# Seven-product blocks in a second FFN of a two-layer diffusion trunk, and the modulation stream over three FFNs

## The chip, the cores and the metric

The kernel runs on one core of one Trainium2 chip. The metric is device time in microseconds (us) of one execution. The kernel before has a median of 1832.51 us over 3 runs (1830.86 to 1833.24).

## The reference

There are two layers. Each has 256 latent tokens and 256 context tokens of width 1024, all in f32, and does the following with shared weights:

```
mod = silu(c) @ ada_w[layer] + ada_b[layer]            # 9 rows of 1024, one set per stream
x   = x + 0.5 * mod[2] * swiglu(ada_rms(x, mod[0], mod[1]))      # FFN 0, width 2816
hx  = ada_rms(x, mod[3], mod[4])
x   = x + mod[5] * mixer(hx, hc)     # neighbourhood attention, gMLP gate, retention
x   = x + 0.5 * mod[8] * swiglu(ada_rms(x, mod[6], mod[7]))      # FFN 1
swiglu(h) = (silu(h @ w1[:, :2816]) * (h @ w1[:, 2816:])) @ w2
```

The context stream goes through the same steps, with its own modulation, up to the mixer of the second layer; only the latent stream is returned. So the second layer needs modulation rows 0 to 4 for both streams, and rows 5 to 8 for one.

## The kernel before

All weights are f32 in memory. A matmul in f32r is made exact enough by splitting each operand into a high and a low part: a weight chunk of 128 x 1024 is loaded into `wr` by SP, copied to `wh` by ScalarE (line 87), and `wl = wr - wh` is made by VectorE (line 98). Each product is then three matmuls: high by high, high by low, low by high (lines 204 to 206). `Stream` (`ws`) keeps three `wr`, four `wh` and four `wl`, and `take` writes the casts and subtractions of two to three chunks ahead of the matmuls that use them.

Names for the stages: FFN (l, f) is FFN f of layer l. Each runs in two halves of eleven blocks. A half has an up stage (eleven blocks j, each one gate and one up column block, 128 columns by 1024 deep, for 512 tokens) and a down stage (eight output tiles m, each of two chunks of 768 and 640 columns). After each m, `residual` (line 429) adds the PSUM result to `xT` on VectorE for the two streams; in the second half `Norm.add` squares the new rows for the next norm (lines 325, 329). In the last half the last two m are split by stream, latent first, and the norm of the latent rows starts (`stats`, line 338, matmuls on PE) while the context half is still running.

The engines' orders are those of the code as it is written (`manual_schedule`). Work that isn't tied to a matmul stands in the list `bg`; `pump` is called after each product and takes `pace[0]` steps from it per 512 columns. `drain_bg` empties it.

FFN (1, 0) computes 18 of its 22 up blocks with `Seven`: the block is a 2 x 2 product (gate and up weights by the two halves of the depth, latent and context tokens), and is made of seven products of half the depth and 256 tokens in place of eight. Its combined weights are made by DMA with accumulation (`add`, on the POOL queue, into `cb`), by POOL (`second`, line 546) and VectorE (`fourth`, line 551), and split as other weights are (lines 531, 540). The four blocks in front (`DIRECT`) are plain, and cover the sums of the activations (`sums`).

The modulation is a stream of matrix-vector products on VectorE: `ada_steps` loads a tile `aw` of 128 x 1024 (512 KB) for each row r and block b, and `step` multiplies and sums it with `cb` (silu of the conditions), once per stream (line 278). A "step" below is one such instruction. Rows 2 to 8 of layer 0 (112 steps) run in FFN (0, 0), all 112 steps of layer 1 in FFN (0, 1). Five `aw` buffers (`ADA_BUFS`) let the load of tile i + 4 be written ahead of step i. The mixer's tables `tab` are loaded once, at the start.

Of the kernel before, what the change touches and what calls it, by code (L numbers as in the profile page):

```python
# [9 lines left out]
F32 = mybir.dt.float32  # L10
# [28 lines left out]
DIRECT = 4  # L39
# [15 lines left out]
APACE = (0.28, 0.26)  # L55
# [77 lines left out]
def tile_hybrid_dit(ctx: ExitStack, tc: tile.TileContext, t_x, t_c, t_cb, t_ada0, t_ada, t_adab, t_nw, t_w1, t_w2,  # L133
# [22 lines left out]
    for l in range(L):  # L156
        for f in range(2):
            if f == 1:
                chunks += [t_wi[l, i] for i in WI[l]] + [t_wo[l, m] for m in range(KT)]
            for half in range(2):  # L160
                for j in range(JH) if (l, f) != (1, 0) else range(DIRECT * (1 - half)):
# [55 lines left out]
    with tc.manual_schedule():  # L217
# [16 lines left out]
        tab = const.tile([128, t_tab.shape[1]], F32, name="tab")  # L234
# [22 lines left out]
        adap = [None]  # L257
        cb = const.tile([128, 2, D], F32, name="cb")

        def ada_steps(l, rounds):  # L260

            todo = [(r, b) for r in rounds for b in range(KT)]
# [10 lines left out]
            def step(i, s, n):  # L273
                loads(i + ADA_BUFS)
                r, b = todo[i]
                t = tiles[r, b]
                junk = adap[0].tile([128, CHUNK], F32, tag="junk", name="junk") if s < n - 1 else t
# [15 lines left out]
            out = [lambda: loads(ADA_BUFS)]  # L293
            for a, r in enumerate(rounds):

                n = 1 if l == L - 1 and r > 4 else 2
                out += [lambda i=a * KT + b, s=s, n=n: step(i, s, n) for b in range(KT) for s in range(n)]
                out.append(lambda r=r, n=n: fin(r, n))
# [149 lines left out]
        class Seven:  # L448
# [8 lines left out]
            def __init__(self, pool, l, f):  # L457
                self.pool, self.l, self.f = pool, l, f
# [4 lines left out]
            def sums(self, q):  # L463
# [3 lines left out]
                def work():  # L467
                    for tag in ("a", "cu", "ur"):
                        x.append(self.pool.tile([128, NT], F32, tag=tag, name="sum", bufs=1).rearrange(
                            "p (k t) -> p k t", k=2))  # L470
# [29 lines left out]
            def load(self, j):  # L500
# [5 lines left out]
                q = cb[:, j % 2]  # L506
# [46 lines left out]
            def prepare(self, j):  # L553
# [4 lines left out]
                        lambda: self.low("r", j)]  # L558
# [15 lines left out]
            def go(self, j, done, nxt):  # L574

                a = self.pool.tile([128, NT], F32, tag="a", name="a", bufs=1)[:, 0:T]
                y = self.pool.tile([128, NT], F32, tag="sg", name="sg", bufs=1)
                w = self.pool.tile([128, NT], F32, tag="cu", name="cu", bufs=1)
# [35 lines left out]
        def ffn(l, f, lead, norms, steps=None, tail=None):  # L614
# [7 lines left out]
            with tc.tile_pool(name="ffn", bufs=1) as fp:  # L622
                adap[0] = fp
                seven = Seven(fp, l, f) if (l, f) == (1, 0) else None
                if seven:
                    caps = [ws.n_take + 2 * DIRECT, ws.n_take + 2 * DIRECT + 2 * KT, len(ws.chunks)]
                    ws.cap = caps[0]
                for half in range(2):
# [34 lines left out]
                    if half == 0 and not one:  # L663
# [10 lines left out]
                        if seven:  # L674
                            bg.extend([s for q in range(2) for s in seven.sums(q)])
                            bg.append(lambda: seven.load_u(DIRECT))
# [8 lines left out]
                    j1 = DIRECT * (1 - half) if seven else JH  # L685
                    if seven and half == 0:
                        seven.load(j1)
                        seven.load(j1 + 1)
                        bg.extend([lambda: seven.add(j1), lambda: seven.add(j1 + 1)])
                        first_j = seven.prepare(j1)  # L690
                    for j in range(j0, j1):
                        if seven and j == j1 - 1:
                            bg.extend(first_j)
# [9 lines left out]
                    if seven:  # L703
                        drain_bg()
                    for j in range(j1, JH if seven else j1):
                        n = half * JH + j

                        def nxt(slot):
                            last_j = j == JH - 1
                            if slot == 1:  # L710
                                seven.high("u", n)
                            if slot == 2:
# [1087 lines left out]
```

## Time and profile before

| | us |
|---|---|
| median of 3 runs | 1832.51 |
| profiled execution, own time | 1833.68 |
| span from its first to last instruction | 1831.9 |
| PE busy in the span | 1802.7 (98%) |
| VectorE busy | 1225.2 (67%) |
| ScalarE busy | 690.0 (38%) |
| POOL busy | 188.0 (10%) |

PE is TensorE's matmuls, DVE is VectorE, ACT is ScalarE. A span is cut into stretches by the stage that runs in it; the busy time of each engine in a stretch tells how much of it is left.

### The profile page before, as it was taken

How to read it: one execution, taken by the hardware profiler on the slowest of the kernel's cores; microseconds unless marked ns; L12 is line 12 of the kernel's file. 1: busy time of each engine (PE TensorE's matmuls, PEld its weight loads, DVE VectorE, ACT ScalarE, POOL GpSimd, SP SyncE). 2: the span in 40 equal slices, each digit the busy share in tenths (PEclk: the TensorE clock that was granted, in tenths of full speed). 3: DMA queues.
4: the chain of work that ended last, by engine and by line, in shares of the span. 5: the costliest groups of instructions: out<-in, count | busy, mean ns of one | idle time of the engine just before them, and what ended most of it. 6: DMA issues, size and time to landing. Idle time of an engine off the chain costs nothing. (4 is left out here: it accounts for less than half of the span.)

```text
span 1831.9 us, 27737 instructions
## 1 busy us (share of the span) xinstructions
PE 1802.7 (98%) x10944; PEld 1534.8 (84%) x10944; DVE 1225.2 (67%) x2064; ACT 690.0 (38%) x1131; POOL 188.0 (10%) x207
## 2 busy tenths in 40 slices
PE   7999999999999999999999999999999999999999
PEld 5788888887668989888888898989998867889999
DVE  5787877756455667877777667846884644566665
ACT  3332222235543234322222234433543555454443
POOL 0000000002024300000000002302320104310000
PEclk9999999999999999999999999999999999999999
DMA  7755655333211124555567425636653432345655
GB/s 287 267 190 185 208 185 198 124 100 115 78 56 58 47 75 153 193 185 182 201 219 266 151 88 150 160 110 175 167 147 96 129 104 77 92 127 182 188 177 156
DMA packets 94242, 277.00 MB, mean 151 GB/s; under 512 B 11040, under 2 KB 17824, under 8 KB 93984
## 3 DMA queue, kind: packets, MB, share of 16 engines
q1 hardware_dynamic: 88928, 265.79, 44.3%
q0 software_dynamic: 5184, 9.44, 3.2%
q8 instruction: 86, 1.41, 0.3%
q14 instruction: 44, 0.36, 0.1%
HBM read 274.14 MB, written 1.05 MB: 150 GB/s over the span
## 5 line engine op out<-in xcount | busy, mean ns | idle before, releaser
L98 DVE TENSOR_TENSOR wl<-wr,wh 128x1024 fp32r<-128x1024 f32 (+1 forms) x340 | 364.5, 1100 | 110.6 <-ACT wh L87 109.1
L87 ACT CAST wh<-wr 128x1024 fp32r<-128x1024 f32 (+1 forms) x340 | 311.8, 945 | 189.2 <-PE d L205 127.6
L204 PE MATMUL d<-aTh,wh 128*128 128x512 f32 (+1 forms) x770 | 268.9, 349 | 0.0
L205 PE MATMUL d<-aTl,wh 128*128 128x512 f32 (+1 forms) x770 | 268.4, 349 | 0.0
L206 PE MATMUL d<-aTh,wl 128*128 128x512 f32 (+1 forms) x770 | 268.4, 349 | 0.0
L204 PE MATMUL g<-hTh,wh 128*128 128x512 f32 (+2 forms) x592 | 208.7, 353 | 2.4 <-ACT wh L87 1.4
L205 PE MATMUL g<-hTl,wh 128*128 128x512 f32 (+2 forms) x592 | 208.4, 352 | 1.3 <-DVE hTl L354 1.1
L206 PE MATMUL g<-hTh,wl 128*128 128x512 f32 (+2 forms) x592 | 207.6, 351 | 1.1 <-DVE wl L98 1.1
L206 PE MATMUL u<-hTh,wl 128*128 128x512 f32 (+2 forms) x592 | 207.4, 350 | 0.4 <-DVE wl L98 0.4
L204 PE MATMUL u<-hTh,wh 128*128 128x512 f32 (+2 forms) x592 | 207.0, 350 | 0.0
L205 PE MATMUL u<-hTl,wh 128*128 128x512 f32 (+2 forms) x592 | 206.9, 349 | 0.0
L205 PEld LDWEIGHTS d<-aTl,wh 128*128 128x128 f32 x770 | 144.5, 188 | 21.3
L204 PEld LDWEIGHTS d<-aTh,wh 128*128 128x128 f32 x770 | 144.5, 188 | 21.2
L206 PEld LDWEIGHTS d<-aTh,wl 128*128 128x128 f32 x770 | 144.5, 188 | 21.2
L278 DVE CUSTOM_DVE_ANT_0 aw<-aw,cb 128x1024 f32<-128x1024 f32 x128 | 155.1, 1223 | 2.4
L652 ACT CAST aTh<-sg 128x512 fp32r<-128x512 f32 x66 | 40.9, 620 | 255.4 <-DVE sg L648 241.7
L212 PE MATMUL nat<-wh,hTh 128*128 128x512 f32 (+2 forms) x384 | 137.1, 357 | 0.0
L429 DVE SCALAR_TENSOR_TENSOR xT<-d,mod,xT 128x256 f32<-128x256 f32 x112 | 50.3, 480 | 122.7 <-PE d L206 122.6
L204 PEld LDWEIGHTS g<-hTh,wh 128*128 128x128 f32 x592 | 111.6, 189 | 20.1 <-ACT wh L87 2.3
L214 PE MATMUL nat<-wh,hTl 128*128 128x512 f32 (+2 forms) x384 | 127.8, 333 | 0.4 <-DVE hTl L354 0.4
L213 PE MATMUL nat<-wl,hTh 128*128 128x512 f32 (+2 forms) x384 | 127.6, 332 | 0.0
L205 PEld LDWEIGHTS g<-hTl,wh 128*128 128x128 f32 x592 | 111.9, 189 | 18.1 <-DVE hTl L354 2.6
(261 smaller groups left out, 3440.4 us busy)
## 6 DMA issues: line engine op xcount, KB each, us to landing
wr<-in_w_dram SPq DMA_DIRECT2D x158, 512.0 KB, 4.3
aw<-in_ada_dram SPq DMA_DIRECT2D x144, 512.0 KB, 5.2
wr<-in_wi_dram SPq DMA_DIRECT2D x56, 512.0 KB, 3.7
wr<-in_w_dram SPq DMA_DIRECT2D x64, 384.0 KB, 3.5
wr<-in_w_dram SPq DMA_DIRECT2D x64, 320.0 KB, 2.9
cb<-in_w_dram SPq DMA_DIRECT2D x36, 256.0 KB, 6.2
cb<-in_w_dram POOLq DMA_DIRECT2D x36, 256.0 KB, 6.2
wr<-in_wo_dram SPq DMA_DIRECT2D x16, 512.0 KB, 3.6
```

Source lines behind the costliest of these rows:

```text
L87: self.nc.scalar.copy(out=h[:, :n], in_=self.raw[i][:, :n])
L98: self.nc.vector.tensor_tensor(out=lo[:, :n], in0=t[:, :n], in1=h[:, :n].bitcast(F32), op=ALU.subtract)
L204: PE.matmul(out=ps, lhsT=wh[:, col:col + 128], rhs=hh[rhs_sl], start=start, stop=False)
L205: PE.matmul(out=ps, lhsT=wh[:, col:col + 128], rhs=hl[rhs_sl], start=False, stop=False)
L206: PE.matmul(out=ps, lhsT=wl[:, col:col + 128], rhs=hh[rhs_sl], start=False, stop=stop)
L212: PE.matmul(out=ps, lhsT=hh[lhs_sl], rhs=wh[:, wc], start=start, stop=False)
L213: PE.matmul(out=ps, lhsT=hh[lhs_sl], rhs=wl[:, wc], start=False, stop=False)
L214: PE.matmul(out=ps, lhsT=hl[lhs_sl], rhs=wh[:, wc], start=False, stop=stop)
L278: V.tensor_tensor_reduce(out=junk, in0=t, in1=cb[:, s], scale=1.0, scalar=0.0, op0=ALU.mult, op1=ALU.add, accum_out=mod[l][:, 8 * r + b, s ...
L429: V.scalar_tensor_tensor(out=xT[:, m, s * T:s * T + T], in0=ps[:, s * T - c0:s * T - c0 + T], scalar=mod[l][:, 24 * i + 16 + m, s:s + 1], ...
L652: S.copy(out=aTh[:, j], in_=sg)
```

## The change

- FFN (0, 1) gets the seven-product form too: four plain blocks, then 18 of seven products.
- Layer 1's 112 modulation steps are spread: 26 behind the 112 of layer 0 in FFN (0, 0), at a pace of 0.34 in place of 0.28; then 18 and 26 in the two down stages of FFN (0, 1); 18 and 24 in the two down stages of FFN (1, 0). (A tile isn't cut in two, so 25 becomes 26, and 24 are left at the end.) The pace of those four is set so that the list is empty behind five of eight m in the first half, seven of eight in the second.
- In FFN (0, 1) and FFN (1, 0) the `aw` tiles have two buffers. They share the tag `aw` with the tiles `q`, which hold what stood in `cb`; `cb` keeps the conditions.
- In a seven-product block `q` and `wr` are loaded one slot earlier in the round, `add` comes earlier, and the subtraction of the next block's gate weights and `second` come behind that of `q`.
- `tab` has its memory in the mixer's pool and is loaded in each mixer, behind its tenth weight load.

```diff
-DIRECT = 4
+DIRECT = {(0, 1): (4, 0), (1, 0): (4, 0)}
+ADA_DOWN = {(0, 1): (18, 25), (1, 0): (18, 25)}
-APACE = (0.28, 0.26)
+APACE = 0.34
...
-        def ada_steps(l, rounds):
-            todo = [(r, b) for r in rounds for b in range(KT)]
+        ada_todo = [[(r, b) for r in range(2 if l == 0 else 0, 9) for b in range(KT)] for l in range(L)]
+        def ada_steps(l, count):
+            def streams(r):
+                return 1 if l == L - 1 and r > 4 else 2
+            todo = []
+            while ada_todo[l] and sum(streams(r) for r, b in todo) < count:
+                todo.append(ada_todo[l].pop(0))
...
-                    t = tiles[r, b] = adap[0].tile([128, CHUNK], F32, tag="aw", name="aw", bufs=ADA_BUFS)
+                    t = tiles[r, b] = adap[0].tile([128, CHUNK], F32, tag="aw", name="aw", bufs=adap[1])
...
             def step(i, s, n):
-                loads(i + ADA_BUFS)
+                loads(i + adap[1])
...
-                q = cb[:, j % 2]
+                q = self.pool.tile([128, CHUNK], F32, tag="aw", name="q", bufs=2)
...
+                def seven_pool():
+                    nonlocal seven
+                    pool = es.enter_context(tc.tile_pool(name="seven", bufs=1))
+                    seven = Seven(pool, fp, l, f)
+                    adap[:] = pool, 2
+                if (l, f) in DIRECT:
+                    seven_pool()
+                elif not one:
+                    adap[:] = fp, ADA_BUFS
...
                         def nxt(slot):
-                            elif slot == 0:
-                                seven.low("g", n + 1)
-                                seven.second(n + 1)
-                                if j < JH - 2:
-                                    seven.load(n + 2)
...
+                            elif slot == 1:
+                                seven.low("u", n)
+                                seven.load_u(n + 1)
+                                if left > 1:
+                                    seven.add(n + 2)
...
                             elif slot == 3:
                                 seven.low("q", n + 1)
-                            elif slot == 4 and j < JH - 2:
-                                seven.add(n + 2)
+                                seven.low("g", n + 1)
+                                seven.second(n + 1)
                             elif slot == 5:
                                 seven.fourth(n + 1)
                                 seven.high("r", n + 1)
+                                if left > 2:
+                                    seven.load(n + 3)
...
+                    if seven:
+                        bg.extend(ada_steps(1, ADA_DOWN[l, f][half]))
+                        pace[0], pace[1] = len(bg) / (JH * (KT - 1 if half else KT - 3)), 0.0
+                    ahead = seven and half == 0
                     for m in range(KT - 2 if split_tail else KT):
...
+                        if ahead and m == KT - 3:
+                            drain_bg()
                             seven.load(JH)
...
+                tab = mp.tile([128, t_tab.shape[1]], F32, tag="tab", name="tab")
...
+                SP.dma_start(out=tab, in_=t_tab)
...
-                bg.extend(ada_steps(0, range(2, 9)))
+                bg.extend(ada_steps(0, 112) + ada_steps(1, 26))
...
-                bg.extend(ada_steps(1, range(9)))
-                pace[0], pace[1] = APACE[1], 0.0
                 ffn(l, 1, "mix", n3, FFN_TO_FFN)
```

The order on the engines moves at three places of which the prediction speaks.

VectorE in the second down stage of FFN (1, 0), around the end of m = 0. Before (L429 is the residual, L98 the two subtractions of the weights of m = 2, L329 the norm's sum):

```order
L429 SCALAR_TENSOR_TENSOR xT<-d,mod_95,xT 128x256 x2
L98 TENSOR_TENSOR wl<-wr,wh 128x768
L98 TENSOR_TENSOR wl<-wr,wh 128x640
L429 SCALAR_TENSOR_TENSOR xT<-d,mod_95,xT 128x256 x2
L329 TENSOR_TENSOR acc<-acc,sq 128x256 x2
```

The same place with the change (L441 is the residual, L100 the subtractions, L341 the norm's sum; a step is the first of each pair of L290):

```order
L441 SCALAR_TENSOR_TENSOR xT<-d,mod_94,xT 128x256 x2
L100 TENSOR_TENSOR wl<-wr,wh 128x768
L100 TENSOR_TENSOR wl<-wr,wh 128x640
L290 ISA aw,mod_94<-aw,cb 128x1024
L290 ISA mod_94 128x1
L290 ISA aw,mod_94<-aw,cb 128x1024
L290 ISA mod_94 128x1
L290 ISA aw,mod_94<-aw,cb 128x1024
L290 ISA mod_94 128x1
L290 ISA aw,mod_94<-aw,cb 128x1024
L290 ISA mod_94 128x1
L441 SCALAR_TENSOR_TENSOR xT<-d,mod_94,xT 128x256 x2
```

Four steps now stand in one piece between the subtractions for one m and the residual of the next. Over the eight groups of the stage (the last two are half as long) there are 2, 4, 3, 4, 3, 4, 3 and 1 of them.

SP's queue in the same stage with the change (L79 is a weight load, L282 an `aw` load):

```order
L79 DMA wr<-in_w_dram 128x640
L79 DMA wr<-in_w_dram 128x768
L282 DMA aw<-in_ada_dram 128x1024 x4
L79 DMA wr<-in_w_dram 128x640
L79 DMA wr<-in_w_dram 128x768
L282 DMA aw<-in_ada_dram 128x1024 x3
```

Each `aw` load is written directly ahead of the step before the one that uses it, and waits for the step that used its buffer last. The first of a group also stands behind the two weight loads, which wait for the two subtractions. Before, this stage's queue held weight loads alone.

VectorE in a seven-product block of FFN (1, 0), from the low part of the last combined weights on. Before:

```order
L540 TENSOR_TENSOR wl<-wr,wh 128x1024
L655 TENSOR_TENSOR aTl<-sg,aTh 128x512
L540 TENSOR_TENSOR wl<-wr,wh 128x1024
L540 TENSOR_TENSOR ul<-ur,uh 128x512
L540 TENSOR_TENSOR wl<-cb,wh 128x1024
L598 TENSOR_TENSOR sg<-p_11550,a 128x512
```

With the change:

```order
L552 TENSOR_TENSOR wl<-wr,wh 128x1024
L680 TENSOR_TENSOR aTl<-sg,aTh 128x512
L552 TENSOR_TENSOR ul<-ur,uh 128x512
L552 TENSOR_TENSOR wl<-q,wh 128x1024
L552 TENSOR_TENSOR wl<-wr,wh 128x1024
L610 TENSOR_TENSOR sg<-p_12094,cu 128x512
```

The gate weights' subtraction now follows that of `q`, and POOL's `second`, which waits for it, now runs beside the instructions that read PSUM (`sg<-p`) and no longer beside the subtraction of `q`.

## Rows read from the trace of the kernel before

**Rows 1.** The page: busy time of the engines over the span.
```profile
PE 1802.7 (98%) x10944; PEld 1534.8 (84%) x10944; DVE 1225.2 (67%) x2064; ACT 690.0 (38%) x1131; POOL 188.0 (10%) x207
```

**Rows 2.** Up stages in windows: stretch, length, busy us of PE, PEld, DVE, ACT, POOL.
```profile
221.20:343.70 122.50, 122.50 (x529) 99.27 (x528) 95.95 (x142) 32.33 (x42) 0.00 (x0) 1.00 0.57 189
...
700.70:828.20 127.50, 126.11 (x636) 105.78 (x636) 101.14 (x161) 41.49 (x59) 0.70 (x1) 1.00 0.56 189
...
889.80:1012.30 122.50, 122.50 (x530) 99.27 (x529) 88.40 (x133) 32.28 (x42) 0.00 (x0) 1.00 0.68 229
...
1125.00:1197.80 72.80, 71.37 (x590) 69.94 (x588) 61.72 (x76) 35.23 (x56) 20.25 (x17) 1.00 0.58 147
...
1259.40:1370.30 110.90, 110.46 (x926) 109.51 (x925) 95.55 (x117) 53.96 (x85) 31.49 (x28) 1.00 0.62 158
```

**Rows 3.** The same of the first 65 us of the last stretch.
```profile
1259.40:1324.60 65.20, 65.20 (x553) 65.20 (x552) 55.31 (x67) 31.40 (x49) 19.84 (x18) 1.00 0.67 172
```

**Rows 4.** Windows: two down stages of FFN (0, 1), second of FFN (1, 0).
```profile
828.20:889.80 61.60, 61.60 (x266) 49.49 (x265) 47.21 (x78) 14.60 (x19) 0.00 (x0) 1.00 0.58 197
...
1012.30:1075.00 62.70, 62.70 (x342) 53.61 (x341) 35.82 (x65) 18.93 (x34) 0.70 (x1) 1.00 0.36 118
...
1370.30:1433.00 62.70, 62.70 (x342) 53.62 (x341) 29.11 (x51) 19.72 (x36) 0.72 (x1) 1.00 0.30 96
```

**Rows 5.** Timeline of DVE, second down stage of FFN (1, 0): start, us, what, [idle before].
```profile
1375.40 0.83 DVE L98 TENSOR_TENSOR wl<-wr,wh 128x640 fp32r<-128x640 f32 x1
...
1408.99 0.88 DVE L429 SCALAR_TENSOR_TENSOR xT<-d,mod,xT 128x256 f32<-128x256 f32 x2 [3.85 <-PE d L206]
1410.02 0.82 DVE L329 TENSOR_TENSOR acc<-acc,sq 128x256 f32<-128x256 f32 x2 [0.15 <-ACT sq L325]
1411.13 1.69 DVE L98 TENSOR_TENSOR wl<-wr,wh 128x768 fp32r<-128x768 f32 x2 [0.30 <-ACT wh L87]
```

**Rows 6.** Timeline of DVE, first down stage of FFN (0, 1).
```profile
844.57 1.69 DVE L98 TENSOR_TENSOR wl<-wr,wh 128x768 fp32r<-128x768 f32 x2
...
851.48 0.88 DVE L429 SCALAR_TENSOR_TENSOR xT<-d,mod,xT 128x256 f32<-128x256 f32 x2 [2.53 <-PE d L206]
...
853.87 1.22 DVE L278 CUSTOM_DVE_ANT_0 junk<-aw,cb 128x1024 f32<-128x1024 f32 x1
...
856.28 1.22 DVE L278 CUSTOM_DVE_ANT_0 junk<-aw,cb 128x1024 f32<-128x1024 f32 x1
```

**Rows 7.** Timeline of SP's queue, the same stage: loads as they are issued.
```profile
845.54 1.07 SPq L77 DMA_DIRECT2D wr<-in_w_dram  x2
846.66 0.42 SPq L270 DMA_DIRECT2D aw<-in_ada_dram  x1
```

**Rows 8.** The `aw` loads of that stage (11 of them), by source line.
```profile
DMA to landing us min/median/max: 4.2/4.9/5.9
```

**Rows 9.** DMA issues from 409 to 450 us, the first mixer: median us to landing last.
```profile
wr<-in_wi_dram SPq DMA_DIRECT2D x9, 512.0 KB, 3.6
```

**Rows 10.** Line 540 by source: xcount: ns min/median/max, first and last start.
```profile
L540 DVE TENSOR_TENSOR wl<-cb,wh x18: 1219/2299/2321, 1124.5 to 1358.1; 128x1024 fp32r<-128x1024 f32 x18
```

**Rows 11.** Timeline of POOL, then of DVE, at one `second`.
```profile
1254.33 1.87 POOL L546 TENSOR_TENSOR wr<-wr,cb 128x512 f32<-128x512 f32 x1
...
1254.06 0.87 DVE L429 SCALAR_TENSOR_TENSOR xT<-d,mod,xT 128x256 f32<-128x256 f32 x2
```

**Rows 12.** What PE's weight loads waited for, 1120 to 1372 us: us, times, longest.
```profile
PEld p L571 <- DVE wl L540: 3.7, 10, 0.8
```

**Rows 13.** PE's timeline at an idle stretch in the second mixer.
```profile
1613.54 0.44 PE L1463 MATMUL yt<-ident,yR 128*128 128x128 f32 x2 [2.54 <-POOL yR L1255]
```

**Rows 14.** The window behind it; the granted clock stands third from the end.
```profile
1614.90:1618.30 3.40, 3.40 (x19) 3.40 (x18) 0.10 (x1) 0.68 (x2) 0.00 (x0) 0.50 0.00 0
```

**Rows 15.** DMA issues: the load of the tables, KB, us to landing.
```profile
tab<-in_tab_dram SPq DMA_DIRECT2D x1, 898.0 KB, 6.8
```

**Rows 16.** First reader of the tables by source: ns, first and last start.
```profile
L1096 DVE TENSOR_SCALAR ww<-lg,tab x8: 224/226/230, 457.5 to 1477.5; 128x6 f32<-128x6 f32 x8
```

More of the change, by code (lines that the diff above doesn't have):

```diff
@@ L160, in tile_hybrid_dit @@
             for half in range(2):
-                for j in range(JH) if (l, f) != (1, 0) else range(DIRECT * (1 - half)):
+                for j in range(DIRECT.get((l, f), (JH, JH))[half]):
                     chunks += [t_w1[l, f, half * JH + j, 0], t_w1[l, f, half * JH + j, 1]]
@@ L291, in fin @@
                     V.tensor_scalar(out=mo, in0=mo, scalar1=0.5, scalar2=None, op0=ALU.mult)
[L293 to L298, printed above, removed]
+            out = [lambda: loads(adap[1])]
+            for i, (r, b) in enumerate(todo):
+                n = streams(r)
+                out += [lambda i=i, s=s, n=n: step(i, s, n) for s in range(n)]
+                if b == KT - 1:
+                    out.append(lambda r=r, n=n: fin(r, n))
             return out
@@ L467, in work @@
                 def work():
[L468 to L470 removed]
+                    t = self.pool.tile([128, CHUNK], F32, tag="cu", name="sum", bufs=1)
+                    u = self.pool.tile([128, NT], F32, tag="ur", name="sum", bufs=1)
+                    x.extend(v.rearrange("p (k t) -> p k t", k=2) for v in (t[:, 0:NT], t[:, NT:2 * NT], u))
                 a, b = slice(0, T), slice(T, NT)
@@ L557, in prepare @@
                         lambda: (self.fourth(j), self.high("r", j)), lambda: self.high("g", j + 1),
-                        lambda: self.low("r", j)]
+                        lambda: (self.low("r", j), self.load(j + 2))]
             def product(self, ps, w, j, k, t):
@@ L621, in ffn @@
             streams = STR[span]
[L622 to L627, printed above, removed]
+            with ExitStack() as es:
+                fp = es.enter_context(tc.tile_pool(name="ffn", bufs=1))
+                seven = None
+                direct = DIRECT.get((l, f), (JH, JH))
+                caps = [ws.n_take + 2 * direct[0], ws.n_take + 2 * sum(direct) + 2 * KT, len(ws.chunks)]
+                caps = [c for c, d in zip(caps, (*direct, 0)) if d < JH]
+                ws.cap = caps.pop(0)
+                def seven_pool():
[7 more added lines that the diff above has]
+                    adap[:] = fp, ADA_BUFS
                 for half in range(2):
@@ L752, in ffn @@
                         ps = mm_bank("d")
-                        if seven and half == 0 and m == KT - 3:
+                        if ahead and m == KT - 3:
+                            drain_bg()
                             seven.load(JH)
@@ L758, in ffn @@
                         down(m, wa, wb, a, b, ps)
-                        if seven and half == 0 and m >= KT - 2:
+                        if ahead and m >= KT - 2:
                             for s in seven.prepare(JH)[slice(0, 4) if m == KT - 2 else slice(4, 7)]:
```

65 lines of the change are left out of this document (32 added, 33 removed).

## The prediction

> **What bounds the kernel now.** I read the page's busy line first: PE 1802.7 us of 1831.9 [rows 1]. Then the windows by stage: the up stages have 122.50 of 122.50 [rows 2], the down stages 61.60 of 61.60 and 62.70 of 62.70 [rows 4], at granted clock 1.00. So there is no idle PE time in the FFNs to take back. A gain must cut matmuls, and whatever makes PE wait there is paid in full. The other engines have room in the mean, VectorE 67%; the windows show where: 95.95 of 122.5 us in a plain up stage with modulation in it, 35.82 and 29.11 of 62.7 in the second down stages. The timelines [rows 5 to 7] show how VectorE's work lies in a down stage, and that is what the sum turns on. The sum is made against the profiled execution, 1833.7 us, which is 1.2 above the median. What a measurement here can tell from no change is about 0.2%, 3.7 us.
>
> **The gain: 18 seven-product blocks in FFN (0, 1).** A plain block takes 122.5 / 11 = 11.14 us [rows 2]. A seven-product block is 84 short matmuls (7 products, 4 tiles of depth, 3 each). Where nothing waits, 553 of them took 65.2 us [rows 3], 0.118 each, so 9.9 us. Over a whole stage it is 110.9 / 11 = 10.1, and over the seven of the first half 72.8 / 7 = 10.4. The rest of that is PE waiting for low parts, ten times, 3.7 us together [rows 12].
>
> At today's rates (0, 1) would gain 7 x 11.14 - 72.8 = 5.2 in the first half and 122.5 - 110.9 = 11.6 in the second: 16.8, the lower bound. At 9.9 it is 78.0 - 70 = 8.0 (a little lead-in left) and 122.5 - 108.9 = 13.6, and FFN (1, 0) gains 2.8 and 2.0: 26.4, the upper. I take **-24**, near the upper, because the order on VectorE removes a visible cost. The low part of `q` takes 2.30 us in the median and 1.22 at best [rows 10]: today it stands beside POOL's `second`. A VectorE pair that reads PSUM took its usual 0.87 beside one [rows 11], and the change puts `second` beside such instructions. One us less per block, out of 55.31 busy in 65.2 [rows 3], is what the low parts are late by.
>
> **The cost: modulation steps in the four down stages.** After each m, VectorE does the residual, in second halves the sum, then the two subtractions for the weights of m + 2; the change puts the steps of the group behind those and ahead of the next residual. Every step is on VectorE's one queue: when it waits for its tile, the next residual, the next norm sum and the next subtractions wait too, and then PE.
>
> Sizes. A step takes 1.2 us (two in 2.41) [rows 6]. The rest of a group, residual to last subtraction, is 3.8 us in a second half (1408.99 to 1412.82) [rows 5], about 2.6 in a first half. A group of four is 3.8 + 4.8 = 8.6 us against PE's 7.7 per m (61.6 / 8) even if no tile is ever late. But there are two buffers, so a tile's load can only start when the step before last has ended. And the first load of each group stands on SP's queue behind two weight loads, which wait for the subtractions: today the subtractions end at 846.26 [rows 6], the weight loads go out at 845.54 and on, the `aw` load at 846.66 [rows 7], 0.4 us behind. Landing takes 4.2 at least and 4.9 in the median in that place [rows 8], 3.6 for a load of 512 KB alone [rows 9]. I take 4.4 for the one behind weight loads, with those 0.4 in front, and 3.6 for the rest.
>
> So a group of four tiles used once (rows 5 to 8 of the second layer) runs: first step at once, second behind the queued load (4.8 + 1.2), third right after it, the fourth's load goes out only as the second step ends and costs another 3.6: 11.0 us. Three take 7.3. Tiles used by two streams get two steps each, and [two, two] takes 7.3.
>
> *FFN (1, 0), second half* (groups 2, 4, 3, 4, 3, 4, 3, 1). The subtractions for m = 1 end 5.9 us into the stage (1370.3 to 1376.23) [rows 4, 5]. VectorE's chain: 5.9; first group done at 13.2; rest 17.1; four 28.1; rest 31.9; three 39.4; rest 43.3; 54.3; 58.1; 65.9; 69.7; 80.7; 84.5; 91.9; last latent residual 95.8. PE by itself is there at 7 x 7.7 = 53.9, and the next norm's `stats` wait for that residual with no slack. **+42**.
>
> *FFN (0, 1), second half* (3, 3, 4, 4, 4, 3, 2, 3; two-stream tiles): the same walk ends at 77.1, **+23**. *FFN (1, 0), first half* (3, 4, 3, 4, 4): there are no sums and three m without steps at the end, but the two groups of four single tiles make PE wait 5 and 6 us for the subtractions of m = 5 and 6: **+13** with the rest. *FFN (0, 1), first half*: **+5**. Together **+83**. The bounds: if each load goes out as its buffer comes free and lands in 3.6, the same walk gives 0, 11, 4 and 25, together 40; with 4.2 for each load and 4.9 behind weights, 99. I take 83, near the upper end, since rows 6 to 8 show the queue's order and landing in just such a stage.
>
> **The other edits.** In FFN (0, 0) there are 26 more steps, 31 us on VectorE. Its second up stage has 122.5 - 95.95 = 26.5 us free and the first is like it; five steps per block fit, six overrun by under a us now and then, which the low parts' lead covers: 0, bound +3. The tables load behind the tenth weight load of a mixer. Even at the end of the stretch in which nine of them go out (450 us), 6.8 us to landing [rows 15] make 456.8, ahead of the first reader at 457.5 [rows 16]; the second mixer has the same order. 0, bound +3 each if the load delays the next weights. The four plain blocks ahead in FFN (0, 1) carry the sums as those of FFN (1, 0) do, in 127.5 - 101.1 = 26 us of free VectorE time [rows 2], with no steps beside them any more: 0. The up stages of (0, 1) lose their steps, which hid beside PE: 0. `q` and `wr` go out a slot earlier and `add` with them; queued ahead of weights in a round of 10 us: 0.
>
> Sum: 1833.7 - 24 + 83 = 1892.7, and **1891.5** on the medians' scale.
>
> **TensorE's clock.** After an idle stretch of 2.54 us in the second mixer [rows 13] the granted clock was 0.50 for 3.4 us, the lower of its two levels [rows 14]: 1.7 us lost. The waits above are of 3 to 7 us per group, so I expect the same behind many of them. In the sum it costs nothing: at 7.7 + 1.7 = 9.4 us PE's m is still shorter than the chain's 11 to 15, so the loss falls into time in which PE would wait. The Trainium skill ("TensorE: Matmul & The Clock Gate", section "HAM oscillation — how this bites in real kernels") speaks against this change more strongly: where compute between two waits for DMA is short, the clock falls at each wait and every tile starts cold. By rows 14 the trace agrees that one wait is enough; that it comes at every wait no row shows.
>
> **The rivals.**
>
> *B: the loads are not held.* Weight loads land and are subtracted early enough that SP's queue is free, or a lone load's 3.6 holds for all. Cost 40: 1833.7 - 24 + 40, **1848.5** on the medians' scale. For: the 3.6 of rows 9. Against: rows 7, where the `aw` load is issued right behind the weight loads as the subtractions end.
>
> *C: faster.* The mechanism is VectorE's lead. Every wait for a tile falls into the time in which VectorE waits for PE anyway: 3.85 us per m in the second halves [rows 5], 2.53 beside two steps in the first [rows 6]. What is left is only occupancy: groups of 8.6 against 7.7, and short last m with 5 and 4 steps, by the walk 8.5 and 6.5 us in the two second halves. 1833.7 - 24 + 15, **1823.5**. It decides at the landing: by the same walk with loads not held, cost and gain meet at about 2 us per load. For: steps ran in a first down stage with PE at 61.60 of 61.60 [rows 4]. Against: that was with five buffers, and no row shows 512 KB landing in 2 us.
>
> *D: the clock at its lower level through whole m.* Then an m is 15.4 us and above the chain. In the two second halves PE alone needs 7 x 15.4 = 107.8, against 95.8 and 77.1: 12 + 31 more, **1934**; in half of the m, 1913. For: rows 13 and 14. Against: behind that wait the clock came back within 3.4 us.
>
> That the change doesn't do what it says, the seven-product blocks staying as they are today, costs 7 us and lies inside the range.
>
> **How the numbers follow.** The forecast 0.64, B 0.15, C 0.12, D 0.08, anything else 0.01. The forecast's own range takes 40 to 99 for the cost and 16.8 to 26.4 for the gain: 1848 to 1915. The range must reach B and part of D: 1846 to 1918, which leaves out C and half of D, 0.16. Faster is C and a part of B in which the gain is larger: 0.13. Within 0.2% takes a cost of 20 to 28, between C and B: 0.02. Slower 0.85.
>
> **What would show it.** Right: steps on VectorE (L290) idle before them for `aw`, some tens of us in all; FFN (0, 1) with up stages of about 120 (four plain, seven others) and 109 us; down stages of about 67, 86, 74 and 105 where 61.6 and 62.7 stand now; PE near 94%; PE's idle time there ended by `wl`; granted clock under 1.00 in those windows. The low part of `q` at 1.22. Wrong: the down stages stay at 62 (then C), or all four grow by ten or less with SP's `aw` loads issued ahead of the weight loads (B); seven-product blocks above 10.1 would cut the gain.

## The result, and the profile after

The changed kernel takes 1924.95 us, the median of 4 runs (1922.04 to 1931.78), beside 1831.68 for the kernel before. The ratio is 1.0515, 95% interval 1.0484 to 1.0547: slower by 5%, and 7 us above the upper end of the range. The forecast was 1891.5.

The profiled execution took 1931.78 us, the slowest of the four; its span is 1929.6. The busy line of its page, against [rows 1]:

```profile
PE 1825.9 (95%) x11592; PEld 1579.8 (82%) x11592; DVE 1312.8 (68%) x2214; ACT 728.7 (38%) x1211; POOL 239.7 (12%) x261
```

PE's busy time went up, though FFN (0, 1) has fewer columns to multiply. The reason stands in the windows of the four down stages, FFN (0, 1) and then FFN (1, 0) (stretch, length, busy us of PE, PEld, DVE, ACT, POOL; third from the end the granted clock):

```profile
830.90:899.60 68.70, 63.91 (x266) 50.41 (x265) 41.60 (x69) 13.13 (x18) 4.86 (x5) 0.98 0.62 189
1011.90:1102.40 90.50, 74.52 (x343) 61.56 (x342) 59.33 (x105) 19.11 (x35) 0.72 (x1) 0.87 0.43 142
1224.70:1305.30 80.60, 66.76 (x267) 51.98 (x266) 42.81 (x71) 13.83 (x18) 4.81 (x5) 0.94 0.61 192
1415.80:1532.30 116.50, 78.28 (x343) 64.32 (x342) 57.65 (x103) 19.11 (x35) 0.71 (x1) 0.79 0.48 160
```

Before, these stages took 61.60 and 62.70 us [rows 4]. They have grown by 7.1, 27.8, 19.0 and 53.8, together 107.7 us. Part of PE's busy time there is the same matmuls at the lower clock. The up stages of FFN (0, 1) and of FFN (1, 0), the same view, against [rows 2]:

```profile
707.90:830.90 123.00, 119.91 (x888) 113.22 (x887) 98.54 (x146) 59.88 (x94) 23.32 (x22) 0.99 0.50 130
899.70:1012.00 112.30, 111.67 (x926) 110.01 (x925) 92.21 (x123) 55.61 (x88) 29.04 (x28) 1.00 0.63 160
1102.50:1224.70 122.20, 118.81 (x888) 112.25 (x887) 99.68 (x147) 58.53 (x93) 23.05 (x22) 1.00 0.52 136
1305.40:1415.80 110.40, 110.22 (x926) 109.50 (x925) 91.00 (x123) 54.86 (x87) 28.86 (x28) 1.00 0.63 161
```

Against 127.5, 122.5, 122.8 (four plain blocks and 72.8) and 110.9 they gain 4.5, 10.2, 0.6 and 0.5: 16 us, not 24. One more stretch differs, in the first mixer:

```profile
616.50:629.50 13.00, 13.00 (x52) 11.58 (x52) 1.69 (x7) 0.90 (x3) 0.36 (x1) 0.50 0.10 36
```

For 13 us the clock was at the lower of its two levels, where the kernel before has 1.00, behind the same short idle of PE (0.67 us here, 0.65 there). It cost 6.5 us: that mixer takes 300.8 us here and 294.3 before. Of the profiles of the experiments none loses more than 1.7 us there, so it belongs to this execution, and explains most of the 6.8 us by which this execution lies above the median. -16 + 107.7 + 6.5, less 1 us elsewhere, is the 97.7 between the two spans.

How a group runs now is on VectorE's timeline in the second half of FFN (1, 0) (start, us, what, [idle before and what ended it]); L441 is the residual, L100 the subtractions, L290 a step:

```profile
1430.88 1.69 DVE L100 TENSOR_TENSOR wl<-wr,wh 128x768 fp32r<-128x768 f32 x2 [1.21 <-ACT wh L89]
1432.49 1.22 DVE L290 CUSTOM_DVE_ANT_0 aw<-aw,cb 128x1024 f32<-128x1024 f32 x1
...
1439.49 1.23 DVE L290 CUSTOM_DVE_ANT_0 aw<-aw,cb 128x1024 f32<-128x1024 f32 x1 [5.78 <-DMA aw<-in_ada_dram]
...
1440.75 1.22 DVE L290 CUSTOM_DVE_ANT_0 aw<-aw,cb 128x1024 f32<-128x1024 f32 x1
...
1444.46 1.23 DVE L290 CUSTOM_DVE_ANT_0 aw<-aw,cb 128x1024 f32<-128x1024 f32 x1 [2.47 <-DMA aw<-in_ada_dram]
...
1445.61 0.87 DVE L441 SCALAR_TENSOR_TENSOR xT<-d,mod,xT 128x256 f32<-128x256 f32 x2
```

The pattern is the one forecast: the first step at once, the second behind a long wait, the third with it, the fourth behind a shorter one. The group of four takes 13.1 us (1432.49 to 1445.61), not 11.0. The residual has no idle before it: VectorE never waits for PE here; the chain is VectorE's and the tiles'. SP's queue at the same place:

```profile
1431.86 1.06 SPq L79 DMA_DIRECT2D wr<-in_w_dram  x2
1432.97 9.37 SPq L282 DMA_DIRECT2D aw<-in_ada_dram  x4
```

The first `aw` load goes out at 1432.97, as the subtractions end, and its step starts at 1439.49: 6.5 us. PE pays behind it. On PE's timeline (same columns):

```profile
1447.70 0.79 PE L206 MATMUL d<-aTh,wh 128*128 128x512 f32 x1 [8.32 <-ACT wh L89]
...
1451.85 0.63 PE L206 MATMUL d<-aTh,wh 128*128 128x512 f32 x1
```

An idle of 8.32 us, matmuls of 0.63 us at the lower clock behind it (granted 0.50 from 1447.70 to 1452.20), then 0.40. The waits listed by engine for that stage (us, times, longest) put the releaser at `wh`, ScalarE's cast. That cast stands behind the square (`sq`) in ScalarE's order, and the square waits for VectorE's residual:

```profile
ACT sq L337 <- DVE xT L441: 80.3, 8, 15.0
DVE aw L290 <- DMA aw<-in_ada_dram: 46.7, 12, 6.2
PEld d L206 <- ACT wh L89: 33.2, 5, 9.9
```

### The profile page after: what moved, and what is told of

It is laid out like the page before. It is cut to its first block, busy times and chain, and to the rows that moved or that the text cites. A ratio compares the mean times of both kernels' runs of the same rounds, so it can differ in the third digit from the quotient of the medians.

```text
span 1929.6 us, 29556 instructions
## 1 busy us (share of the span) xinstructions
PE 1825.9 (95%) x11592; PEld 1579.8 (82%) x11592; DVE 1312.8 (68%) x2214; ACT 728.7 (38%) x1211; POOL 239.7 (12%) x261
## 5 line engine op out<-in xcount | busy, mean ns | idle before, releaser
L100 DVE TENSOR_TENSOR wl<-wr,wh 128x1024 fp32r<-128x1024 f32 (+2 forms) x304 | 322.1, 1086 | 109.4 <-ACT wh L89 108.6
L89 ACT CAST wh<-wr 128x1024 fp32r<-128x1024 f32 (+2 forms) x304 | 275.6, 932 | 207.4 <-DMA wr<-in_w_dram 97.8
L290 DVE CUSTOM_DVE_ANT_0 aw<-aw,cb 128x1024 f32<-128x1024 f32 x128 | 156.6, 1223 | 65.4 <-DMA aw<-in_ada_dram 62.5
L207 PE MATMUL g<-hTl,wh 128*128 128x512 f32 (+2 forms) x448 | 151.5, 338 | 1.3 <-DVE hTl L366 1.1
L208 PE MATMUL u<-hTh,wl 128*128 128x512 f32 (+2 forms) x448 | 150.6, 336 | 0.5 <-DVE wl L100 0.5
L206 PE MATMUL u<-hTh,wh 128*128 128x512 f32 (+2 forms) x448 | 150.3, 336 | 0.0
L207 PE MATMUL u<-hTl,wh 128*128 128x512 f32 (+2 forms) x448 | 150.3, 335 | 0.0
L290 DVE CUSTOM_DVE_ANT_0 junk<-aw,cb 128x1024 f32<-128x1024 f32 x96 | 117.1, 1220 | 41.1 <-DMA aw<-in_ada_dram 40.6
L583 PE MATMUL p<-hTh,wl 128*128 128x256 f32 x432 | 124.1, 287 | 1.6 <-DVE wl L552 0.5
L583 PE MATMUL p<-th,wl 128*128 128x256 f32 x432 | 122.0, 282 | 0.2 <-DVE wl L552 0.2
L582 PE MATMUL p<-hTl,wh 128*128 128x256 f32 x432 | 121.4, 281 | 0.0
```

What stands on the lines that cost most here:

```text
L89: self.nc.scalar.copy(out=h[:, :n], in_=self.raw[i][:, :n])
L100: self.nc.vector.tensor_tensor(out=lo[:, :n], in0=t[:, :n], in1=h[:, :n].bitcast(F32), op=ALU.subtract)
L206: PE.matmul(out=ps, lhsT=wh[:, col:col + 128], rhs=hh[rhs_sl], start=start, stop=False)
L207: PE.matmul(out=ps, lhsT=wh[:, col:col + 128], rhs=hl[rhs_sl], start=False, stop=False)
L208: PE.matmul(out=ps, lhsT=wl[:, col:col + 128], rhs=hh[rhs_sl], start=False, stop=stop)
L290: V.tensor_tensor_reduce(out=junk, in0=t, in1=cb[:, s], scale=1.0, scalar=0.0, op0=ALU.mult, op1=ALU.add, accum_out=mod[l][:, 8 * r + b, s ...
```

## The experiments

Two theories stood against each other. Theory 1: VectorE waits for tiles, because with two buffers the second tile of each group is loaded behind the weight loads. Theory 2: the steps' own time on VectorE and the lower clock are the cost. Each kernel is the changed one with the edit shown. Four of them (e1, e2, e4, e7) ran once: their time stands beside the median of the kernel before on the same chip, without an interval, and the windows of their profiles carry the argument. The others have intervals.

### Loads written behind the step (e1_load_behind)

```diff
                                        accum_out=mod[l][:, 8 * r + b, s:s + 1])
+                if adap[1] == 2 and s == n - 1:
+                    loads(i + adap[1] + 1)
```

> The changed kernel with each `aw` load of the down stages written right behind the step that frees its buffer, instead of ahead of the step before its use: the first two tiles of a group are then loaded while the group before is still being closed, ahead of the two weight loads in SP's queue. Theory 1 (VectorE waits for tiles, because the second tile of every group is loaded behind the weight loads): a group of four single tiles falls from 13.1 us to about 8 (two steps at once, the third tile 3.6 us behind the first step's end, the fourth with it), one of three from 9.2 to about 6; the down stages lose some 60 of their 108 us, time about 1865 us (1850 to 1885). Theory 2 (the steps' own time on VectorE and the clock at its lower level are the cost, not the order of loads): 1910 to 1930.

Measured: 1878.5 us beside 1828.5. The down stages, in windows:

```profile
823.10:885.70 62.60, 61.69 (x265) 49.34 (x264) 41.36 (x69) 13.29 (x18) 4.84 (x5) 1.00 0.66 207
997.90:1075.90 78.00, 69.06 (x341) 57.70 (x340) 58.87 (x105) 19.02 (x35) 0.72 (x1) 0.93 0.50 164
1198.30:1271.10 72.80, 64.12 (x265) 50.28 (x265) 43.33 (x73) 13.89 (x18) 4.81 (x5) 0.98 0.67 211
1381.70:1480.50 98.80, 73.80 (x341) 60.30 (x340) 57.08 (x103) 18.96 (x35) 0.71 (x1) 0.88 0.56 188
```

They are 63.6 us above those of before: 44 of the 107.7 us were the place of the loads in SP's queue, where theory 1 gave some 60. Theory 2 falls. The time is 13 us above what theory 1 gave, but inside its bounds. VectorE's timeline, a group of four:

```profile
1421.68 1.22 DVE L290 CUSTOM_DVE_ANT_0 aw<-aw,cb 128x1024 f32<-128x1024 f32 x1
...
1422.83 1.22 DVE L290 CUSTOM_DVE_ANT_0 aw<-aw,cb 128x1024 f32<-128x1024 f32 x1
...
1427.34 1.22 DVE L290 CUSTOM_DVE_ANT_0 aw<-aw,cb 128x1024 f32<-128x1024 f32 x1 [3.28 <-DMA aw<-in_ada_dram]
...
1430.05 0.87 DVE L443 SCALAR_TENSOR_TENSOR xT<-d,mod,xT 128x256 f32<-128x256 f32 x2
```

Four take 8.4 us now (8 expected). A group of three takes 7.5 (1410.46 to 1418.00 in the same timeline), not 6: its third tile is loaded only as the first step ends, and VectorE sits idle for 3.8 us before it all the same. What two buffers can't hold is still waited for.

### One tile for all steps (e2_one_tile)

```diff
                 while nload[0] < min(n, len(todo)):
+                    if adap[1] == 2 and nload[0]:
+                        tiles[todo[nload[0]]] = tiles[todo[0]]
+                        nload[0] += 1
+                        continue
...
-                junk = ... if s < n - 1 else t
+                junk = ... if s < n - 1 or adap[1] == 2 else t
```

> The changed kernel, but all steps of a down stage read one tile that is loaded once (the modulation rows made there are wrong): no wait for a tile, the same VectorE time. Theory 1: what is left is occupancy, about 15 us, all in the two second halves: up stages -16, down stages +15, time about 1831 us (1825 to 1840), granted clock near 1.00 in the down stages. Theory 2: 1880 or more.

This kernel leaves out every load of a down stage but the first. Measured: 1841.3 us beside 1828.5, just above the expected band. The down stages, in windows:

```profile
996.90:1073.30 76.40, 68.39 (x342) 56.23 (x342) 59.42 (x105) 19.20 (x35) 0.72 (x1) 0.96 0.26 86
1369.80:1441.80 72.00, 66.50 (x342) 55.66 (x341) 57.53 (x103) 19.11 (x35) 0.71 (x1) 0.95 0.28 91
823.70:885.30 61.60, 61.60 (x266) 49.55 (x265) 41.78 (x69) 13.68 (x18) 4.86 (x5) 1.00 0.49 145
1195.60:1259.30 63.70, 61.82 (x266) 49.45 (x265) 43.53 (x72) 13.89 (x18) 4.81 (x5) 1.00 0.47 144
```

25 us are left (13.7, 9.3, 0, 2.1), where 15 were worked out. What those 15 (8.5 in the second half of FFN (0, 1), 6.5 in that of FFN (1, 0)) lacked is the first tile, for which this kernel still waits. In the stage of 76.40 us the first step waits 5.11 us for it, until 1007.42, 5.1 us behind the subtractions that end at 1002.3; the groups of four that follow are each longer than PE's m, so nothing recovers that lead. So 83 of the 107.7 us are waits for tiles behind the first, with what the lower clock costs behind them. (The forecast's 83 is another sum: it holds occupancy and the first tile too. That the two are equal is chance.)

### No loads, and steps of 16 columns, in the down stages (e3_no_steps)

```diff
-                while nload[0] < min(n, len(todo)):
+                while adap[1] > 2 and nload[0] < min(n, len(todo)):
...
+                if adap[1] == 2:
...
+                    V.tensor_tensor_reduce(out=junk[:, 0:16], in0=cb[:, s, 0:16], in1=cb[:, s, 0:16], ...)
+                    return
```

> The changed kernel with the steps of the four down stages cut to 16 columns of the conditions and without their loads (leaves these modulation rows out): the gain of the seven-product blocks alone. By the up stages of the changed kernel's profile (-4.5, -10.2, -0.5, -0.4) 1832 - 16 = 1816 us (1813 to 1819), down stages at 61.6 and 62.7. If the up stages suffer from what the down stages leave behind (late buffers, late weights), and the prediction's 9.9 us per block is right without it: 1808. If the slow stretch in the first mixer (granted clock 0.50 for 13 us) belongs to the change: 6 us more.

Measured: 1814.3 us (median of 4 runs) beside 1828.5, ratio 0.9915, 95% interval 0.9899 to 0.9932. The down stages are back at 61.6 and 62.7, and the first mixer has no slow stretch. The seven-product blocks of the change are worth some 15 us by the runs, 17 by the up stages of this profile (123.1, 110.5, 122.3 and 110.5); the 24 of the prediction were not hidden by what the down stages leave behind.

### The gate's low part first (e4_gate_first)

```diff
-                                seven.low("q", n + 1)
                                 seven.low("g", n + 1)
                                 seven.second(n + 1)
+                                seven.low("q", n + 1)
```

> The changed kernel with the gate weights' low part and POOL's `second` ahead of the low part of `q` (the rest of the order as changed). By contention: `q`'s low part takes 2.3 us again beside `second`, VectorE's round gets 1.1 us longer, and the later blocks of a stage go from 10.3 to 10.5 us or more: up stages of seven products +2 us or more each. By order (PE waits 0.34 us per block for the gate's low part, which stands last): that wait goes, blocks of 9.93 us to the end of the stage, -3 us in each long stage. Down stages as in the changed kernel.

Measured: 1918.1 us beside 1828.5. The theory of the order holds, with less gain in the long stages than its 3 us. In the changed kernel the second part of a long up stage runs below PE's rate, and here it doesn't (windows; the changed kernel's from 1370.6, this kernel's from 1357.2 on):

```profile
1370.60:1415.80 45.20, 45.02 (x374) 44.30 (x373) 37.52 (x51) 22.54 (x38) 9.37 (x9) 1.00 0.56 137
```

```profile
1357.20:1401.10 43.90, 43.90 (x374) 43.90 (x373) 37.19 (x50) 21.03 (x35) 12.12 (x8) 1.00 0.53 147
```

The same 374 matmuls take 45.20 and 43.90 us. On VectorE's timeline of the changed kernel the gate's low part (`wl<-wr`) is the last before the next block, and the starts of `sg<-p` show the round:

```profile
1385.20 0.69 DVE L610 TENSOR_TENSOR sg<-p,cu 128x512 f32<-128x512 f32 x1
...
1394.36 1.22 DVE L552 TENSOR_TENSOR wl<-wr,wh 128x1024 fp32r<-128x1024 f32 x1
1395.50 0.68 DVE L610 TENSOR_TENSOR sg<-p,cu 128x512 f32<-128x512 f32 x1
```

The round is 10.30 us. The gate's low part ends at 1395.58, and PE's first matmul with it (`hTh,wl`) starts at 1395.64:

```profile
1395.31 0.28 PE L582 MATMUL p<-hTl,wh 128*128 128x256 f32 x1
1395.64 0.39 PE L583 MATMUL p<-hTh,wl 128*128 128x256 f32 x1
```

It starts 0.33 us behind the one before, where these matmuls otherwise follow each other by 0.12. A block's first product uses the gate weights, its second `q`; so with the gate first, PE needs `q`'s low part only a product later. The up stages are 121.9, 109.7, 119.8 and 109.2. Against the changed kernel the long ones (second and fourth) gain 2.6 and 1.2 us, where 3 were expected. Against the kernel before all four are 23 us less: the 24 of the prediction, but by this order and not by the change's.

The other theory named a cost that didn't come: `q`'s low part stayed at 1.22 us at most, and POOL's `second` took 2.15 us in its place (by source, the two kernels' long stages of FFN (1, 0): first the changed one, then this one):

```profile
L558 POOL TENSOR_TENSOR wr<-wr,q x10: 1282/1291/1296, 1313.3 to 1406.0; 128x512 f32<-128x512 f32 x10
```

```profile
L558 POOL TENSOR_TENSOR wr<-wr,q x10: 1860/2148/2156, 1298.6 to 1388.1; 128x512 f32<-128x512 f32 x10
```

### Half of each tile loaded (e7_half_tile)

This asks why the second tile of a group landed only after 6.4 us.

```diff
-                    SP.dma_start(out=t, in_=t_ada[l, r, b])
+                    SP.dma_start(out=t[:, 0:512], in_=t_ada[l, r, b][:, 0:512])   # in the down stages
...
+                    for k in range(2):
+                        V.tensor_tensor_reduce(out=junk[:, 512 * k:512 * k + 512], in0=t[:, 0:512],
+                                               in1=cb[:, s, 512 * k:512 * k + 512], ...)
```

> The changed kernel with half of each `aw` tile loaded in the down stages (256 KB), and each step as two instructions over that half (rows made there are wrong; the time on VectorE stays about 1.3 us per step). Disputed: why a load behind two weight loads landed after 6.4 us here and after 4.9 in the kernel before. If it is bytes in flight together (two weight loads, two tiles): they are then those of the kernel before, the second tile lands after about 4.9, the fourth after 2.6 (3.6 for 512 KB), the group of four falls from 13.1 to about 11, down stages from +108 to +75 or 85, 1890 to 1900 us. If it is a fixed delay of the queue: landing stays at 6 or more, and so do 1915 to 1930 us.

In the down stages this kernel leaves out half of each tile. Measured: 1905.9 us beside 1832.1, down stages 66.7, 90.2, 75.1 and 105.5, +89. The time lies between the two bands. A group of four on VectorE's timeline (two instructions per step):

```profile
1440.90 0.69 DVE L295 CUSTOM_DVE_ANT_0 junk<-aw,cb 128x512 f32<-128x512 f32 x1
...
1445.15 0.69 DVE L295 CUSTOM_DVE_ANT_0 junk<-aw,cb 128x512 f32<-128x512 f32 x1 [3.55 <-DMA aw<-in_ada_dram]
...
1449.35 0.69 DVE L295 CUSTOM_DVE_ANT_0 junk<-aw,cb 128x512 f32<-128x512 f32 x1 [1.30 <-DMA aw<-in_ada_dram]
```

The load that went out at 1440.66 is used at 1445.15, 4.5 us where it was 6.5, and the waits for tiles in that stage fall from 46.7 to 30.0 us. So a fixed delay of the queue is out, and the bytes decide. Half of these 2 us is the tile's own size: the fourth tile, with no weight load in front, lands after 2.6 us here and after 3.6 with 512 KB. The other half goes with what is in flight beside it. The sums of bytes agree: from the first weight load of the group shown above (1431.86) to the landing of the third tile (1433.74, 6.9 us after) 1728 KB land in 8.8 us; here 1216 KB land in some 6 us, from 1439.55. The gain on the whole is smaller than expected (1890 to 1900). Each step costs 1.45 us as two instructions, not 1.3, which is of that sign; how much of the miss it makes isn't shown.

### Three versions with the steps spread (e5_spread, e6_balance, e8_balance2)

By the runs so far a down stage should carry two-step tiles that two buffers can hold, loaded behind the step. All three have the loads of e1, the gate first as in e4, and the first two loads of a stage written at its start.

```diff
-        ada_todo = [[... for r in range(2 if l == 0 else 0, 9) ...] for l in range(L)]
+        ada_todo = [[... for r in ((2, 3, 4, 5, 6, 7, 8), (5, 6, 7, 8, 0, 1, 2, 3, 4))[l] ...] for l in range(L)]
-ADA_DOWN = {(0, 1): (18, 25), (1, 0): (18, 25)}
+ADA_DOWN = {(0, 1): (16, 16), (1, 0): (16, 16)}
...
-                        bg.extend(ada_steps(1, ADA_DOWN[l, f][half]))
+                        first_loads, *rest = ada_steps(1, ADA_DOWN[l, f][half])
+                        first_loads()
+                        bg.extend(rest)
+                        pace[1] = -JH * pace[0]
...
-                bg.extend(ada_steps(0, 112) + ada_steps(1, 26))
+                bg.extend(ada_steps(0, 112) + ada_steps(1, 48))
```

> Loads behind the step, the gate's low part ahead of that of `q`, and the steps spread by what the runs so far show: rows 5 to 8 (one step per tile) and row 0 of the second layer go into FFN (0, 0), where five buffers hold (48 steps in place of 26, pace 0.38); each down stage keeps 16 steps of two-step tiles, none in its first m, groups of four in a first half (4.8 + 2.6 us against 7.7), of two to three in a second (3.6 + 3.8). If tiles and occupancy are the whole cost: up stages -23 as with the gate first, down stages of FFN (0, 1) and (1, 0) within 2 us of 61.6 and 62.7 each, FFN (0, 0) +0 to 4 for its fuller VectorE: about 1811 us (1804 to 1818), faster than both kernels. If steps in a down stage cost something by themselves (clock, queue): 5 us and more in each, 1825 or above.

Measured: 1824.0 us (median of 6 runs) beside 1829.1, ratio 0.9969 (0.9957 to 0.9982), above the expected 1804 to 1818. The up stages gain 23, and all four down stages are at 61.6 and 62.7 with 16 steps in each: a step in a down stage costs nothing by itself. But FFN (0, 0), with 48 steps of layer 1 in it, loses 1.0, 2.7, 5.1 and 7.5 us in its four stages, four times the 4 us that were expected at most.

The next version takes 12 of them back, with rows 5 to 7 in front and row 8 last, 20, 16, 20 and 20 steps, and a pace for each stage of FFN (0, 0):

```diff
-(5, 6, 7, 8, 0, 1, 2, 3, 4)
+(5, 6, 7, 0, 1, 2, 3, 4, 8)
...
-                bg.extend(ada_steps(0, 112) + ada_steps(1, 48))
+                bg.extend(ada_steps(0, 112) + ada_steps(1, 36))
...
+                    elif lead == "start":
+                        pace[0] = (0.364, 0.273)[half]
```

> As the spread kernel, with the 16 us that FFN (0, 0) lost there (1.0, 2.7, 5.1, 7.5 by stage, from its profile) taken back: 36 steps of the second layer there in place of 48 (rows 5 to 7 and a part of row 0), a pace per stage so that a group in a second half has three steps and not four; the down stages take 20 and 16 in FFN (0, 1), 20 and 20 in FFN (1, 0), steps in the first m too. If VectorE's occupancy sets what FFN (0, 0) loses: +3 to 5 there, 0 to 2 in each down stage, 4 in the last one (single tiles of row 8 in groups of three): about 1814 us (1809 to 1819). If FFN (0, 0) loses by its number of loads and not by VectorE's time (36 steps need more loads than 26): +10 there, 1820.

Measured: 1817.7 us (median of 6 runs) beside 1832.1, ratio 0.9924 (0.9911 to 0.9937): inside the expected band, and 0.8% below the kernel before. The first three down stages are 61.5, 62.6 and 61.5 us in windows; the last:

```profile
1347.00:1417.20 70.20, 64.85 (x341) 55.27 (x340) 51.08 (x93) 18.69 (x34) 0.71 (x1) 0.98 0.56 184
```

FFN (0, 0) is within 1 us of before. The last stage, with eight tiles used once, loses 7.6 us, nearly twice what was expected.

The last one moves those tiles into FFN (0, 0) (40 steps there; 20, 20, 18 and 14 in the down stages, pace 0.35):

> As the balanced kernel, but all tiles with one step (rows 5 to 8) in FFN (0, 0), 40 steps there, 20 and 20 in FFN (0, 1), 18 and 14 in FFN (1, 0), all of two-step tiles. If groups of three single tiles with two buffers cost the 7.6 us that the last down stage of FFN (1, 0) lost in the balanced kernel: that stage back to 63, FFN (0, 0) +1 to 3 for four more steps: about 1812 us (1808 to 1816) beside 1829 to 1832. If that stage lost by the number of its steps (20): +3 there and the same in the second half of FFN (0, 1), no gain over the balanced kernel.

Measured: 1818.3 us (median of 6 runs) beside 1830.9, ratio 0.9928 (0.9917 to 0.9940), just above the expected 1808 to 1816. The last stage is back at 62.7, and that of FFN (0, 1), with 20 steps of two-step tiles, is 63.3, so it was the single tiles and not the number of steps. The time comes back elsewhere: the last stage of FFN (0, 0) takes 69.4 and the first down stage of FFN (1, 0) 65.2, so this version is no better than the one before it. In that down stage the groups no longer begin with a new tile: a group of four ends on the first step of a third one, which two buffers can't hold, and waits 1.7 to 2.2 us for it. In the last stage of FFN (0, 0) the tiles used once outrun even five buffers: just ahead of it VectorE waits 2.2 us for one, PE then waits 2.7 us behind that for `aTh`, and runs 6.8 us at 0.50 after it, which costs 3.4 us more.

## Why the prediction was wrong

The direction and the mechanism were right: the down stages lose more than the blocks gain, and VectorE's waits for tiles, with weights, residuals and PE behind them, are what they lose it to. The time lies above the range because the cost was taken 25 us too small (83, and it was 107.7) and the gain 8 us too large (24, and it was 16). Both err to the same side, and together they are the 33 us between 1891.5 and 1924.95.

- **"I take 4.4 for the one behind weight loads."** This is the step that failed. In the last stage, in the six groups behind the first, that load landed after 5.7 to 6.9 us, after 6.4 in the group shown. The row the 4.4 came from, 4.2 at least and 4.9 in the median [rows 8], had one tile in flight behind two weight loads. Here the first step of a group of single tiles runs at once and frees its buffer, so the next load goes out 0.8 us behind, and both share the transfer. With half the bytes the same load was used after 4.5. In the second half of FFN (0, 1), with two-step tiles, the next load goes out 2.0 us later, and the one behind the weights landed after 5.0 to 5.8: sooner, but not after 4.4 either. The source view of the loads, all of a stage together, for the second half of FFN (0, 1), then of FFN (1, 0):

```profile
DMA to landing us min/median/max: 3.6/5.0/5.8
...
DMA to landing us min/median/max: 3.5/5.6/7.3
```

  Some 2 us in each of those six groups are the last stage's 54 against 42. In the second half of FFN (0, 1) the groups of four took 8.2, 7.9 and 8.5 us where the walk has 7.3, which is over half of its 28 against 23. In the first half of FFN (1, 0) the two groups of four took 12.4 and 13.2 us, not 11.0: about 4 of the 6 us of its 19 against 13. The bound of 99 took 4.9 at most, and so was no bound.

- **Occupancy and the first tile.** The 15 us of rival C left out the first tile of a stage; one tile for all steps still waits for it and leaves 25. The forecast's own walk had it, 4.8 us behind the subtractions, and that was right: in the changed kernel VectorE is idle for 4.3 to 4.7 us before the first step of a stage.

- **"I take -24, near the upper."** The change gives 16 in its profile and 15 to 17 without the steps, about the lower bound of 16.8. The visible cost did go: `q`'s low part is at 1.23 us throughout, as expected [rows 10]. But the new order puts the gate's low part last, and PE needs it first, so a stop of some 0.3 us per block takes the place of the old one. A cost removed from a chain was counted as a gain without asking what is last on it now. With the two swapped the block is at 9.9 us and the gain 23.

- **The other edits at nothing:** FFN (0, 0) took 139.6 us in its first up stage (138.95 before) and the same as before in the other three; the tables cost nothing that the profiles show, as the first mixer takes 294.3 us in the kernels e2 to e4, as before. Right.

- **The clock.** It fell in all four down stages, to 0.79 in the last, and a wait of 8.32 us was followed by matmuls of 0.63 us. The rule of the Trainium skill ("TensorE: Matmul & The Clock Gate", section "HAM oscillation — how this bites in real kernels") agrees with this trace in the main: the granted clock is below 1.00 in each of the four stages, by how much the waits are long (0.98 for 7 us lost, 0.79 for 54). It didn't fall at every wait: behind one of 2.72 us, before PE's matmul at 1460.60, it stayed at 1.00. The clock was costed at nothing, and in the last stage the residuals without idle before them show this: VectorE, not PE, ends each m. Where no steps follow, it isn't free. In the first half of FFN (1, 0) PE's last wait ends at 1288.77, and PE then runs to the end of the stage by itself, its first 3.3 us at 0.50 (the same view of windows):

```profile
1288.70:1292.00 3.30, 3.23 (x8) 2.56 (x9) 2.40 (x5) 0.38 (x1) 0.00 (x0) 0.50 0.64 192
```

  That is some 1.6 us of the 19.0. Rival D, PE itself as the bound, did not come. Rival B is out by SP's queue as it stands in the profile after, rival C by the 107.7 us.

- **A slip in the range.** A cost of 40 with a gain of 26.4 gives 1846, not 1848. Nothing hangs on it.

## What to carry to other kernels

A load that shares a tag of two buffers can be written ahead of its use by one tile only; if it is written behind the step that frees the buffer, it goes out before the queue's next blocking loads, and that alone was worth 44 us here. Work put on an in-order engine between a result and what waits for it must come in portions that its buffers hold when the portion begins, or every late load holds everything queued behind it. A landing time taken from a row holds only for the bytes in flight beside it in that row, and where a wait on a chain is removed, name the instruction that is last then, before counting the gain.

## What the runs showed of the hardware

When an instruction of VectorE and one of POOL overlap and neither reads PSUM, in the pairs looked at the one that starts later is stretched, and ends about when it would if it began at the end of the other. Before, `second` on POOL starts at 1347.43, while VectorE works on `ul`, and VectorE's subtraction for `q` (in `cb`) starts at 1347.82 (timelines of VectorE and of POOL):

```profile
1347.21 0.68 DVE L540 TENSOR_TENSOR ul<-ur,uh 128x512 fp32r<-128x512 f32 x1
1347.82 2.32 DVE L540 TENSOR_TENSOR wl<-cb,wh 128x1024 fp32r<-128x1024 f32 x1
```

```profile
1347.43 1.62 POOL L546 TENSOR_TENSOR wr<-wr,cb 128x512 f32<-128x512 f32 x1 [7.06 <-DVE wl L540]
```

`ul` ends at 1347.89; with 1.29 us, which `second` takes without such company, that makes 1349.18 for its end, and it ends at 1349.05. From there the subtraction with its usual 1.22 would end at 1350.27, and it ends at 1350.14. With the gate first, the subtraction starts at 1348.11 and `second` 0.22 us behind it:

```profile
1348.11 1.22 DVE L552 TENSOR_TENSOR wl<-q,wh 128x1024 fp32r<-128x1024 f32 x1
```

```profile
1348.33 2.15 POOL L558 TENSOR_TENSOR wr<-wr,q 128x512 f32<-128x512 f32 x1 [1.61 <-issue]
```

VectorE's instruction is now unstretched, and POOL's ends at 1350.48, where 1349.33 and 1.29 make 1350.62. In the changed kernel, beside VectorE's `sg<-p` and `cu<-p`, which read PSUM, `second` stays at 1.29. Beside the residuals of [rows 11], which read PSUM too, it took 1.87, so what it shares with which instruction is open. And the clock can stay at its lower level for 13 us behind an idle of PE of 0.67 us in one execution and not at all in others of the same instructions; what decides it no run here shows.
